# Eight softmax scalings and one diagonal moved from GpSimd to VectorE in a one-core decoder block

## The chip, the cores and the metric

The kernel runs on one core of one Trainium2 chip. The metric is the device time of one launch in microseconds (us). Five engines work side by side, each through its own list of instructions in a fixed order: TensorE (PE; its weight loads, PEld, have rows of their own), VectorE (DVE), ScalarE (ACT), GpSimd (POOL) and SyncE (SP), which here only issues transfers. An instruction that waits holds up all that stand behind it on its engine.

## The reference

One decoder block over 256 tokens of width 1024: norm, one q/k/v projection, two groups of eight attention heads, output projection, squared-ReLU MLP, a gated per-layer embedding, final norm. What the change touches is the norm ahead of the projection and the softmax of both groups:

```python
hn = rmsnorm(h, g_attn[i])            # y = x * rsqrt(mean(x*x) + EPS), times a gain
qkv = hn @ w_in[i]
...
scores = jnp.where(valid, scores + bias, -jnp.inf)      # group A, three dilations merged
lse = jax.nn.logsumexp(scores, axis=-1)
probs = jnp.exp(scores - lse[..., None])
...
sc = jnp.where(mask, sc - slopes * dist, -jnp.inf)      # group B
pr = jax.nn.softmax(sc, axis=-1)
out = jnp.einsum('bhqjk,bhqjkd->bhqd', pr, vg)
```

With 256 tokens each head's softmax is over at most 256 keys, so the kernel does it in two pieces of 128 queries (one with 256 keys, one with 128).

## The kernel before, in words

Every large product is done three times in fp32r: the operands are split into `hi` and `lo` halves and `mm3` (lines 151 to 155) multiplies hi by hi (L153), hi by the other's lo (L154) and lo by hi (L155). Weights arrive in slabs of 1 MB. Splitting a slab is cut into pieces: ScalarE makes `hi` (L75), VectorE makes `lo` from it (L76, `SCALAR_TENSOR_TENSOR`). The work is a list of units. While TensorE runs the steps of one unit, the pieces of the next unit's slabs are made. `inserts` names what is put between the steps: in `{4: [x_stats], 12: [x_bcast, ...]}` the statistics of x come behind step 4 and their broadcast behind step 12. An automatic scheduler then fixes the order of each engine's list.

**The diagonal.** GpSimd sums the squares of x (L253, L254) into `xsq`. `x_stats` adds them over the features on TensorE (L260), VectorE scales the sums (L185), GpSimd raises them to the power -1/2 (L186), and GpSimd multiplies the identity by the result, two tiles of 128x128 called `diag` (L267). `x_bcast` multiplies these on TensorE (L273) and VectorE copies the product to `rb` (L274), which scales every q and k (L287, L288). In the first q/k unit two output columns run side by side over k = 0 to 7. Steps 9 and 10 are the first to read the second of the unit's two slabs; its four `lo` pieces are made by VectorE directly behind L185.

**The scalings.** Heads go in pairs (g, j), group g = 0 or 1 and j = 0 to 3, eight pairs from (0,0) to (1,3). For a pair, `evac_qk` makes q and k with their halves (L287 to L294), `scores` multiplies them on TensorE (L316), VectorE adds the bias and takes the extremes (L322, L325), ScalarE does four exponentials with their sums (L331), VectorE takes the reciprocal of the four sums (L333), and GpSimd multiplies the four pieces of the probabilities `pb` by it in place (L337: 128x256 and 128x128 for each of two heads). `turn` then transposes `pb` on TensorE, three tiles for each head (L347), and `values` multiplies by v (L359, L360). GpSimd also makes the bias tables for later pairs (L304, and L306 for group 0), and those stand in its list between the scalings.

Of the kernel before, what the change touches and what calls it, by code (L numbers as in the profile page):

```python
# [14 lines left out]
ALU = mybir.AluOpType  # L15
# [17 lines left out]
def block_kernel(ctx: ExitStack, tc: tile.TileContext, a: dict):  # L33
    nc = tc.nc
# [8 lines left out]
    def bank():  # L43
        n_ps[0] += 1
        return psum.tile([P, 512], F32, tag="ps", name=f"ps{n_ps[0]}")
# [136 lines left out]
    def rstd_of(sums, n, width):  # L182

        ms, r = st(n), st(n)
        nc.vector.tensor_scalar(ms, sums, 1.0 / width, EPS, op0=ALU.mult, op1=ALU.add)  # L185
        nc.gpsimd.tensor_tensor(r, ms, mhalf[:, :n], op=ALU.pow)  # L186
        return r
# [35 lines left out]
    ident = outer.tile([P, P], F32, name="ident")  # L223
# [17 lines left out]
    xr = {}  # L241
# [14 lines left out]
    def sum_tokens(sums):  # L256

        ps = bank()
        for t in range(2):
            nc.tensor.matmul(ps[:, t : t + 1], sums[:, t * P : (t + 1) * P], ones[:, :1], start=True, stop=True)  # L260
        return ps[:, :2]

    def x_stats():
        xr["r"] = rstd_of(sum_tokens(xsq), 2, DM)
        diag = ap.tile([P, 2, P], F32, name="diag")
        for t in range(2):
            nc.gpsimd.tensor_scalar(diag[:, t], ident, xr["r"][:, t : t + 1], 1.0, op0=ALU.mult, op1=ALU.mult)  # L267
        xr["diag"] = diag

    def x_bcast():  # L270
# [37 lines left out]
    def scores(g, j):  # L308
        d = pr[g, j]

        ps = [bank(), bank()]
        for c, w, q0 in ((0, S, P), (S, P, 0)):
            for i, (a_, b_) in enumerate(((0, 0), (0, 1), (1, 0))):
                for h in range(2):
                    r = slice(h * HD, (h + 1) * HD)
                    last_mm[0] = nc.tensor.matmul(ps[h][:, c : c + w], d["q"][a_][r, q0 : q0 + P], d["k"][b_][r, :w],  # L316
                                                  start=i == 0, stop=i == 2)
        sc = ap.tile([P, 2, 3 * P], F32, tag="sc", name="sc", bufs=2)
        pb = d["p"] = ap.tile([P, 2, 3 * P], F32, tag="pb", name="pb", bufs=2)
        nm = ap.tile([P, 3, 4], F32, tag="nm", name="nm", bufs=3)  # L320
        for h in range(2):
            nc.vector.tensor_tensor_reduce(  # L322
                sc[:, h, P:], ps[h][:, :S], biases[g, j][:, h], 1.0, 3e38,
                op0=ALU.add, op1=ALU.min, accum_out=nm[:, 0, 2 * h : 2 * h + 1])
            nc.vector.tensor_tensor_reduce(  # L325
                sc[:, h, :P], ps[h][:, S : S + P], biases[g, j][:, h, P:], 1.0, 3e38,
                op0=ALU.add, op1=ALU.min, accum_out=nm[:, 0, 2 * h + 1 : 2 * h + 2])
        for h in range(2):
            for i, sl in ((0, slice(P, 3 * P)), (1, slice(0, P))):
                c = slice(2 * h + i, 2 * h + i + 1)  # L330
                nc.scalar.activation(pb[:, h, sl], sc[:, h, sl], AF.Exp, bias=nm[:, 0, c], scale=-1.0,  # L331
                                     accum_out=nm[:, 1, c])
        nc.vector.reciprocal(nm[:, 2], nm[:, 1])  # L333
        for h in range(2):
            for i, sl in ((0, slice(P, 3 * P)), (1, slice(0, P))):
                c = slice(2 * h + i, 2 * h + i + 1)
                nc.gpsimd.tensor_scalar(pb[:, h, sl], pb[:, h, sl], nm[:, 2, c], 1.0,  # L337
                                        op0=ALU.mult, op1=ALU.mult)

    def turn(g, j):  # L340
        d = pr[g, j]
# [84 lines left out]
    E_ = lambda g, j: (lambda: evac_qk(g, j, *qk_ps[g, j]))  # L426
    B_ = lambda g, j: (lambda: make_bias(g, j))
    S_ = lambda g, j: (lambda: scores(g, j))
    T_ = lambda g, j: (lambda: turn(g, j))
    V_ = lambda g, j: (lambda: values(g, j))  # L430
# [327 lines left out]
```

## Time and profile before

| | us |
|---|---|
| median of 3 runs | 351.51 (349.98 to 351.67) |
| the profiled execution, whole time | 348.54 |
| its span in the trace | 346.8 |
| TensorE busy | 331.6 (96%) |
| VectorE busy | 221.6 (64%) |
| ScalarE busy | 198.3 (57%) |
| GpSimd busy | 91.0 (26%) |

The profiled execution was 348.54 us, of which 1.7 us lie outside its span; it is 0.8% under the median of the three timed runs. The busy shares are means over stages: VectorE's 64% is made of stretches with over 90% and others with under half. Attention, where the change is, runs from about 23 to 105 us; from there on the products of the output projection and the MLP follow. Where the trace says that an engine waited for another, the row names the last of the events it waited for.

### The profile page before, as it was taken

The page shows a single profiled execution, that of the slowest core. Times are in us where ns is not written, and L with a number is a line of the kernel's source. Part 1 is how long each engine was busy: PE and PEld are TensorE (multiplying, and loading weights), DVE is VectorE, ACT ScalarE, POOL GpSimd, SP SyncE. Part 2 cuts the span into 40 slices and gives each one's busy share as a digit, 9 for nine tenths or more (in the row PEclk, how much of TensorE's full clock was granted, in tenths as well). Part 3 has the DMA queues.
Part 4 walks back from the last instruction along what each step waited for, and adds up shares of the span by engine and source line. Part 5 has one row for each costly group of instructions (what it writes and reads, how often), then busy time and mean ns, then how long its engine had stood idle before and what let it go on. Part 6 is the DMA issues. An engine that isn't in the chain of part 4 may idle for free.

```text
span 346.8 us, 5629 instructions
## 1 busy us (share of the span) xinstructions
PE 331.6 (96%) x2188; PEld 296.6 (86%) x2188; DVE 221.6 (64%) x371; ACT 198.3 (57%) x370; POOL 91.0 (26%) x120
## 2 busy tenths in 40 slices
PE   7899999999989999999999999999999999999990
PEld 6689889999866889898998988989989899888890
DVE  4898999786855669637537275293553843757563
ACT  5676667785783668738345374372652825458431
POOL 1887574554222001311010110110201102000443
PEclk9899999999999999999999999999999999999997
DMA  6996844435264078563737618356194472700011
GB/s 180 370 381 227 316 160 135 159 123 194 94 241 154 15 241 315 200 231 106 259 124 239 246 38 327 124 169 259 58 322 163 133 246 107 242 2 0 2 61 61
DMA packets 10827, 60.87 MB, mean 176 GB/s; under 512 B 1200, under 2 KB 1968, under 8 KB 4016
## 3 DMA queue, kind: packets, MB, share of 16 engines
q1 hardware_dynamic: 10800, 60.51, 49.5%
q8 instruction: 17, 0.28, 0.3%
q14 instruction: 10, 0.08, 0.1%
HBM read 59.46 MB, written 1.05 MB: 174 GB/s over the span
## 4 chain that ended last, share of the span: by engine, by line
PE 81%; POOL 7%; DVE 5%; ACT 2%; issue 2%; DMA 2%; SPq 1%; POOLq 0%; DVEq 0%; ACTq 0%
PE ps L153 26%; PE ps L154 25%; PE ps L155 25%; DVE lo L76 3%; POOL xsq L254 2%; POOL pb L337 2%; DMA xT<-in_xT 2%; POOL sq L253 1%; PE ps L359 1%; PE ps L316 1%; PE ps L347 1%; ACT pb L331 1%; PE ps L476 1%; PE ps L360 1%; SPq L212 0%
## 5 line engine op out<-in xcount | busy, mean ns | idle before, releaser
L76 DVE SCALAR_TENSOR_TENSOR lo<-raw,head,hi 128x512 fp32r<-128x512 f32 (+2 forms) x137 | 109.8, 851 | 24.3 <-ACT hi L75 24.2
L75 ACT ACTIVATE hi<-raw,head 128x512 fp32r<-128x512 f32 (+2 forms) x137 | 92.6, 734 | 26.0 <-PE ps L154 11.2
L153 PE MATMUL ps<-hhi,hi 128*128 128x256 f32 x256 | 72.6, 283 | 0.0
L155 PE MATMUL ps<-hhi,lo 128*128 128x256 f32 x256 | 72.4, 283 | 0.0
L154 PE MATMUL ps<-hlo,hi 128*128 128x256 f32 x256 | 72.4, 283 | 0.0
L84 DVE TENSOR_TENSOR lo<-raw,hi 128x1024 fp32r<-128x1024 f32 x34 | 41.5, 1254 | 28.1 <-ACT hi L83 28.0
L540 POOL TENSOR_TENSOR sq<-r 128x512 f32<-128x512 f32 (+1 forms) x18 | 19.9, 1107 | 141.8 <-ACT r L538 141.8
L153 PE MATMUL ps<-hi,u 128*128 128x512 f32 x128 | 50.2, 392 | 0.0
L83 ACT ACTIVATE hi<-raw 128x1024 fp32r<-128x1024 f32 x34 | 34.3, 1052 | 27.2 <-PE ps L155 25.5
L154 PE MATMUL ps<-lo,u 128*128 128x512 f32 x128 | 49.9, 390 | 0.0
L155 PE MATMUL ps<-hi,u 128*128 128x512 f32 x128 | 49.8, 389 | 0.0
L153 PEld LDWEIGHTS ps<-hhi,hi 128*128 128x128 f32 x256 | 49.1, 192 | 0.3
L154 PEld LDWEIGHTS ps<-hlo,hi 128*128 128x128 f32 x256 | 49.1, 192 | 0.3
L155 PEld LDWEIGHTS ps<-hhi,lo 128*128 128x128 f32 x256 | 49.1, 192 | 0.0
L153 PE MATMUL ps<-xhi,hi 128*128 128x256 f32 x128 | 37.8, 297 | 0.0
L154 PE MATMUL ps<-xlo,hi 128*128 128x256 f32 x128 | 36.0, 282 | 0.0
L155 PE MATMUL ps<-xhi,lo 128*128 128x256 f32 x128 | 35.4, 282 | 0.0
L543 DVE TENSOR_TENSOR u<-sq,u 128x512 fp32r<-128x512 f32 (+1 forms) x18 | 11.7, 651 | 34.0 <-ACT u L542 34.0
L155 PEld LDWEIGHTS ps<-hi,u 128*128 128x128 f32 x128 | 24.0, 188 | 5.0
L153 PEld LDWEIGHTS ps<-hi,u 128*128 128x128 f32 x128 | 24.1, 188 | 4.7
L154 PEld LDWEIGHTS ps<-lo,u 128*128 128x128 f32 x128 | 24.1, 188 | 4.7
L153 PEld LDWEIGHTS ps<-xhi,hi 128*128 128x128 f32 x128 | 24.4, 191 | 1.2 <-issue 0.7
(128 smaller groups left out, 540.2 us busy)
## 6 DMA issues: line engine op xcount, KB each, us to landing
raw<-in_w_up SPq DMA_DIRECT2D x16, 1024.0 KB, 5.0
raw<-in_w_down SPq DMA_DIRECT2D x16, 1024.0 KB, 4.8
raw<-in_w_in SPq DMA_DIRECT2D x10, 1024.0 KB, 6.3
raw<-in_w_out SPq DMA_DIRECT2D x4, 1024.0 KB, 4.8
raw<-in_w_gate SPq DMA_DIRECT2D x4, 1024.0 KB, 4.9
raw<-in_w_in SPq DMA_DIRECT2D x7, 256.0 KB, 6.7
h_sb<-in_x SPq DMA_DIRECT2D x1, 1024.0 KB, 7.2
raw<-in_w_ple SPq DMA_DIRECT2D x1, 1024.0 KB, 4.9
```

What stands on the lines that cost most here:

```text
L75: nc.scalar.activation(h, r, AF.Copy, scale=sc)
L76: nc.vector.scalar_tensor_tensor(l, r, sc, h.bitcast(F32), op0=ALU.mult, op1=ALU.subtract)
L83: nc.scalar.activation(h, r, AF.Copy)
L84: nc.vector.tensor_tensor(l, r, h.bitcast(F32), op=ALU.subtract)
L153: nc.tensor.matmul(ps, lhs[0], rhs[0], start=start, stop=False)
L154: nc.tensor.matmul(ps, lhs[0], rhs[1], start=False, stop=False)
L155: last_mm[0] = nc.tensor.matmul(ps, lhs[1], rhs[0], start=False, stop=stop)
L253: nc.gpsimd.tensor_tensor(sq, x, x, op=ALU.mult)
L254: nc.gpsimd.tensor_tensor(xsq, xsq, sq, op=ALU.add)
L337: nc.gpsimd.tensor_scalar(pb[:, h, sl], pb[:, h, sl], nm[:, 2, c], 1.0, op0=ALU.mult, op1=ALU.mult)
L540: nc.gpsimd.tensor_tensor(sq, r, r, op=ALU.mult)
L543: nc.vector.tensor_tensor(o[1], sq, o[0].bitcast(F32), op=ALU.subtract)
```

## The change

The two multiplications of the identity and the four multiplications of each pair's probabilities are issued on VectorE, as `tensor_scalar` with one operation (the form on GpSimd had a second multiplication by 1.0):

```diff
         for t in range(2):
-            nc.gpsimd.tensor_scalar(diag[:, t], ident, xr["r"][:, t : t + 1], 1.0, op0=ALU.mult, op1=ALU.mult)
+            nc.vector.tensor_scalar(diag[:, t], ident, xr["r"][:, t : t + 1], None, op0=ALU.mult)
...
                 c = slice(2 * h + i, 2 * h + i + 1)
-                nc.gpsimd.tensor_scalar(pb[:, h, sl], pb[:, h, sl], nm[:, 2, c], 1.0,
-                                        op0=ALU.mult, op1=ALU.mult)
+                nc.vector.tensor_scalar(pb[:, h, sl], pb[:, h, sl], nm[:, 2, c], None, op0=ALU.mult)
```

GpSimd loses 34 instructions and VectorE gains 34; every shape stays. TensorE's list and the transfers keep their order. Lines behind the edit carry a number that is lower by one.

VectorE, about the statistics of x (`stat` holds them, `lo` are the pieces of weight slabs, `rb` the broadcast):

```order
 L76 SCALAR_TENSOR_TENSOR lo<-raw,head,hi 128x512 x5
 L185 TENSOR_SCALAR stat<-ps_303 128x2
+L267 TENSOR_SCALAR diag<-ident,stat 128x128 x2
 L76 SCALAR_TENSOR_TENSOR lo<-raw,head,hi 128x512 x4
 L274 COPY rb<-ps_339 128x256
```

The two diagonal products, which need the result of GpSimd's L186, now stand ahead of the four `lo` pieces of the second slab.

VectorE, from the softmax of pair (0,0) on (`q` and `k` are those of pair (0,1), `nm` holds the sums and their reciprocals):

```order
 L292 TENSOR_TENSOR q<-q 128x256
 L333 RECIPROCAL nm<-nm 128x4
+L337 TENSOR_SCALAR pb<-pb,nm 128x256
+L337 TENSOR_SCALAR pb<-pb,nm 128x128
+L337 TENSOR_SCALAR pb<-pb,nm 128x256
+L337 TENSOR_SCALAR pb<-pb,nm 128x128
 L294 TENSOR_TENSOR k<-k 128x256
 L76 SCALAR_TENSOR_TENSOR lo<-raw,head,hi 128x512 x5
```

The four scalings follow the reciprocal and stand ahead of the `lo` half of the next pair's k and of five slab pieces.

GpSimd, the same place (bias tables and scalings of group 0):

```order
 L304 TENSOR_SCALAR bias<-consts 128x256 x2
 L306 TENSOR_TENSOR bias<-bias,consts 128x256 x2
-L337 TENSOR_SCALAR pb<-pb,nm 128x256
-L337 TENSOR_SCALAR pb<-pb,nm 128x128
-L337 TENSOR_SCALAR pb<-pb,nm 128x256
-L337 TENSOR_SCALAR pb<-pb,nm 128x128
 L304 TENSOR_SCALAR bias<-consts 128x256 x2
 L306 TENSOR_TENSOR bias<-bias,consts 128x256 x2
```

GpSimd's scalings stood behind the bias table of a later pair; now its list holds the bias tables one after the other.

## Rows read from the trace of the kernel before

**Rows 1.** Page, part 1: busy us, share, instructions of each engine

```profile
PE 331.6 (96%) x2188; PEld 296.6 (86%) x2188; DVE 221.6 (64%) x371; ACT 198.3 (57%) x370; POOL 91.0 (26%) x120
```

**Rows 2.** TensorE's waits, whole span: us in total, times, longest

```profile
PE ps L347 <- POOL pb L337: 2.8, 3, 1.2
PE ps L153 <- ACT xhi L219: 2.4, 2, 1.8
PE ps L164 <- DVE mhalf L174: 1.0, 1, 1.0
PE ps L260 <- POOL xsq L254: 0.8, 1, 0.8
```

**Rows 3.** Waits of TensorE's weight loads, 20 to 124 us, one row

```profile
PEld ps L273 <- POOL diag L267: 0.3, 1, 0.3
```

**Rows 4.** Timeline of TensorE: start us, us, instructions [idle before <- releaser]

```profile
25.29 0.40 PE L155 MATMUL ps<-xhi,lo 128*128 128x256 f32 x2
...
26.01 0.40 PE L155 MATMUL ps<-xhi,lo 128*128 128x256 f32 x2
26.49 0.83 PE L273 MATMUL ps<-diag,ones 128*128 128x128 f32 x4
...
40.50 0.91 PE L316 MATMUL ps<-k,q 64*128 64x256 f32 x12
42.38 0.55 PE L347 MATMUL ps<-ident,pb 128*128 128x128 f32 x3 [0.43 <-POOL pb L337]
44.04 0.55 PE L347 MATMUL ps<-ident,pb 128*128 128x128 f32 x3 [1.11 <-POOL pb L337]
...
97.75 0.55 PE L347 MATMUL ps<-ident,pb 128*128 128x128 f32 x3
99.52 0.55 PE L347 MATMUL ps<-ident,pb 128*128 128x128 f32 x3 [1.22 <-POOL pb L337]
```

**Rows 5.** Timeline of GpSimd, same columns

```profile
23.70 1.17 POOL L186 TENSOR_TENSOR stat<-stat,mhalf 128x2 f32<-128x2 f32 x1 [0.94 <-DVE stat L185]
24.98 1.81 POOL L267 TENSOR_SCALAR diag<-ident,stat 128x128 f32<-128x128 f32 x2
26.87 0.89 POOL L304 TENSOR_SCALAR bias<-consts 128x256 f32<-128x256 f32 x2
...
39.04 1.61 POOL L306 TENSOR_TENSOR bias<-bias,consts 128x256 f32<-128x256 f32 x2
40.65 3.34 POOL L337 TENSOR_SCALAR pb<-pb,nm 128x256 f32<-128x256 f32 x4
...
54.37 2.48 POOL L337 TENSOR_SCALAR pb<-pb,nm 128x256 f32<-128x256 f32 x4 [0.72 <-DVE nm L333]
...
96.87 2.60 POOL L337 TENSOR_SCALAR pb<-pb,nm 128x256 f32<-128x256 f32 x4 [7.34 <-DVE nm L333]
```

**Rows 6.** Timeline of VectorE, same columns

```profile
17.77 5.55 DVE L76 SCALAR_TENSOR_TENSOR lo<-raw,head,hi 128x512 fp32r<-128x512 f32 x5
23.46 0.16 DVE L185 TENSOR_SCALAR stat<-ps 128x2 f32<-128x2 f32 x1
23.54 2.74 DVE L76 SCALAR_TENSOR_TENSOR lo<-raw,head,hi 128x512 fp32r<-128x512 f32 x4
...
39.10 0.18 DVE L333 RECIPROCAL nm<-nm 128x4 f32<-128x4 f32 x1 [0.40 <-ACT pb L331]
39.41 0.65 DVE L294 TENSOR_TENSOR k<-k 128x256 fp32r<-128x256 f32 x1
40.03 4.50 DVE L76 SCALAR_TENSOR_TENSOR lo<-raw,head,hi 128x512 fp32r<-128x512 f32 x5
...
96.53 0.18 DVE L333 RECIPROCAL nm<-nm 128x4 f32<-128x4 f32 x1 [0.76 <-ACT pb L331]
97.94 2.59 DVE L76 SCALAR_TENSOR_TENSOR lo<-raw,head,hi 128x1024 fp32r<-128x1024 f32 x2 [1.24 <-ACT hi L75]
```

**Rows 7.** VectorE's groups by shape: busy us, mean ns of one | idle before

```profile
L677 DVE TENSOR_SCALAR hg<-hg,stat 128x512 f32<-128x512 f32 x2 | 1.0, 488 | 1.3 <-POOL stat L675 1.3
L185 DVE TENSOR_SCALAR stat<-ps 128x2 f32<-128x2 f32 x3 | 0.5, 155 | 1.8 <-PE ps L260 1.6
```

**Rows 8.** Timeline of the end of the kernel: VectorE and GpSimd side by side

```profile
342.37 0.49 DVE L677 TENSOR_SCALAR hg<-hg,stat 128x512 f32<-128x512 f32 x1 [0.67 <-POOL stat L675]
342.44 0.75 POOL L680 TENSOR_SCALAR hg<-hg,stat 128x256 f32<-128x256 f32 x1
```

**Rows 9.** Three stretches of attention: us, busy us (instructions) of each engine, clock

```profile
40.00:55.00 15.00, 13.46 (x118) 12.17 (x118) 13.82 (x37) 10.68 (x32) 10.86 (x17) 1.00 0.64 227
...
sum 44.00, PE 42.46 PEld 39.12 DVE 37.15 ACT 31.21 POOL 26.82; mean PE 14.15 PEld 13.04 DVE 12.38 ACT 10.40 POOL 8.94
```

**Rows 10.** The chain that ended last, one piece: transposes of pair (0,2)

```profile
60.05 0.66 PE ps L347 x6
```

## Prediction

> **What bounds the kernel now.** I read the page's busy shares first: TensorE works 331.6 of 346.8 us [rows 1], so a change elsewhere can only give back time in which TensorE stands still, or cost some. Next its waits over the whole span [rows 2]: four kinds, 7.0 us together. Two of these belong to the start (x's split, the warm-up) and one to the sum of squares ahead of the statistics; the change leaves them alone. The fourth, 2.8 us in three waits, is for the scaled probabilities. The weight loads add 0.3 us in front of the diagonal's product [rows 3]. So the most that this change can take away directly is 2.8 + 0.3 = 3.1 us. The timeline shows where the three are [rows 4]: 0.43 and 1.11 us at the transposes of pair (0,0), 1.22 us at those of pair (1,3). The other six pairs have none: pair (0,2), for one, is scaled by 54.37 + 2.48 = 56.85 us and transposed at 60.05 [rows 5, 10]. From about 105 us on TensorE has no wait among the four, so what is won by then should stay won to the end.
>
> **Part 1, the scalings.** For pair (0,0) the reciprocal is done at 39.10 + 0.18 = 39.28 us [rows 6], but GpSimd first finishes a later bias table (39.04 + 1.61 = 40.65), then scales for 3.34 us, to 43.99 [rows 5]: 4.7 us after the reciprocal. For pair (1,3) nothing is queued ahead, and it is 2.60 us from 96.87 on, to 99.47, 2.8 us after the reciprocal's end at 96.71.
>
> No scaling on VectorE is in the trace. The nearest rows are its two `tensor_scalar` forms [rows 7]: 155 ns for 128x2 and 488 ns for 128x512. On a line between them, 128x128 is 155 + 333 x 126/510 = 237 ns and 128x256 is 155 + 333 x 254/510 = 321 ns, so a pair's four are 2 x 0.237 + 2 x 0.321 = 1.12 us. If every one cost what the smaller row or the larger one costs, it is 0.62 or 1.95 us. I take 1.12, since both shapes lie between the rows and operation and engine are the same; only the source of the smaller row, PSUM, differs.
>
> Pair (0,0) is then scaled at about 39.28 + 1.12 = 40.4 us, before the 41.95 us at which TensorE would reach its transposes (42.38 - 0.43). Both waits go: **-1.54 us**. Pair (1,3): 96.71 + 1.12 = 97.83. The first head's half is done by 97.27, ahead of 97.75, and the second head's by 97.83, while TensorE would reach it near 98.30 (99.52 - 1.22). That wait goes too: **-1.22 us**. The list behind it is not hurt there, since the pieces at 97.94 idled 1.24 us for ScalarE anyway [rows 6]. What is late next at both places is nothing but TensorE's own list.
>
> The cover: the other six pairs gain nothing, and add 1.12 us each to VectorE. In 40 to 84 us VectorE is busy 37.15 of 44 us [rows 9], so 6.85 us are free; six pairs add 6.7. What makes it fit is that VectorE is slowed by GpSimd today: five slab pieces beside the scalings of pair (0,0) took 4.50 us, 0.90 each, against 2.74/4 = 0.69 at 23.54 us [rows 6], so that pair gives back 5 x 0.21 = 1.1 us. And the transposes have room: 3.2 us for pair (0,2), as above. I cost these six at nothing. If that cover were gone, they would cost what is over, which is the last rival below.
>
> One thing behind the scalings is tight: the k half of pair (0,1) (L294), whose scores start at 40.50 us. It ended at 39.41 + 0.65 = 40.06; behind the scalings and without its own slowing it ends at about 40.4 + 0.4 = 40.8. Part 2 moves TensorE's need to about 41.2, so I put +0.1 us here, between nothing and the rival's 1.2.
>
> By the Trainium skill ("SBUF — State Buffer", section "Who interferes with whom") a VectorE `tensor_scalar` in its two-port mode and a GpSimd instruction exclude one another: the one that starts first keeps the shared ports for its whole length. The trace agrees at the one place that shows it: a GpSimd 128x256 that started 0.07 us after VectorE's 0.49 us `tensor_scalar` took 0.75 us [rows 8], against 0.89/2 = 0.45 each for the bias tables of that shape [rows 5]. That speaks against the move wherever GpSimd still makes bias tables; the sum by it is the second rival's.
>
> **Part 2, the diagonal.** It saves GpSimd 1.81 us, and the 0.3 us that TensorE's weight load waited. But look at VectorE's list: the two products now stand between L185 and four slab pieces, and they need GpSimd's power, done at 23.70 + 1.17 = 24.87 us [rows 5]. Before, VectorE started those pieces at 23.54 and did not wait [rows 6]. Now it stands still from 23.62 to 24.87, and the first piece comes after 24.87 + 2 x 0.24 + 0.69 = 26.04 us instead of 24.23. TensorE's first use of that piece is the L155 pair at 25.29 us, the next piece's is at 26.01 [rows 4]. So there is **a new wait**. In addition GpSimd, free of the diagonal, starts its bias tables at 24.87 instead of 26.87 and runs beside VectorE's pieces; pieces beside GpSimd took 0.90 (above) to 5.55/5 = 1.11 us [rows 6]. I take 0.25 us more: 26.3, that is 1.0 us after 25.29. Bounds: diagonal products of 0.155 us and a piece of 0.69 give 25.87, +0.6 us; products of 0.488, a bias operation of 0.45 in front and a piece of 1.11 give 27.4, +2.1, and as pieces 1.11 apart are used 0.72 apart, the second costs 0.4 more: +2.5. I stay near the lower end, because the pieces at 23.54 themselves ran at 0.69 while GpSimd's diagonal tried to run beside them. With the 0.3 us gone at the diagonal's own product, part 2 costs **+0.7 us** (0.3 to 2.2).
>
> **Sum.** -1.54 - 1.22 + 0.1 + 0.7 = -1.96, say -2.0 us. The profiled execution took 348.54 us (346.8 of span), so 346.5 us. The timed runs lie higher, median 351.51; the same ratio, 346.5/348.54 = 0.9943, gives 349.5 us, which I predict.
>
> **Rivals.**
> *The diagonal costs more.* If the pieces come 1.11 us apart, part 2 is +2.2 and the sum -2.76 + 0.1 + 2.2 = -0.5: 348.1 profiled, 351.0 median. For it: pieces at 17.77 us did run at 1.11 [rows 6]. Against: those ran beside two-input GpSimd work.
> *GpSimd's bias tables block the scalings.* At pair (0,0) the two L306 take 1.61 us. If the four scalings wait out both, they end at 39.28 + 1.61 + 1.12 = 42.0 and the k half at 42.4, against scores wanted at 41.2: +1.2 in place of +0.1, sum -0.9, 347.6 profiled, 350.6 median. Against: the bias tables start earlier now too.
> *No new wait.* If another instruction or a later need hides the first piece, only 0.3 is gained in part 2: -3.0, 348.5 median. Against: the order and the 25.29 us row leave no cover.
> *The move does not remove the waits,* because exponentials or something else end last at the same place: then part 2 alone counts, +0.7, 352.2 median. Against: the reciprocal was done 4.7 and 2.8 us before the scalings ended.
> *VectorE becomes the bound, and it is slower.* With 1.95 us for a pair, six add 11.7 us to 37.15: 48.9 in 44, 4.9 us too many, and -2.0 + 4.9 = +2.9: 351.4 profiled, 354.4 median. It decides once a pair costs over 6.85/6 = 1.14 us net of what GpSimd's absence gives back. For it: 13.82 of 15 us are busy from 40 to 55 [rows 9]. Against: the 3 us of room, and the slowing that goes.
>
> **How the numbers follow.** Chances: forecast 0.52, costlier diagonal 0.15, blocked scalings 0.12, no new wait 0.08, waits stay 0.05, VectorE bound 0.08. About 0.5% (1.75 us) is what a measurement of this kernel can tell from no change. The forecast lies just beyond that bound, so its 0.52 splits into 0.38 faster and 0.14 same; no new wait is all faster; the costlier diagonal and the blocked scalings are 0.25 same and 0.02 faster; waits that stay count 0.04 same and 0.01 slower; the bound VectorE is slower. Faster 0.48, same 0.43, slower 0.09. The range takes in the forecast with its bounds, both dearer cases and the missing wait, with about 0.4 us for the spread of runs: 347.9 to 351.6.
>
> **What would show it.** Right: no wait of L347 for the scalings; VectorE idle about 1.25 us in front of the diagonal, by GpSimd's power; a new wait of TensorE's L155 near 25.3 us of about 1 us, for a slab piece; scalings of 0.24 and 0.32 us; slab pieces near 41 us at about 0.7. Wrong: L155 near 25.3 without a wait, scores (L316) waiting for the k half from 40 us on, or VectorE without idle time from 40 to 84 us while TensorE waits for it.

## The result, and the profile after

The changed kernel takes 347.47 us (median of six runs, 347.12 to 348.55), against 350.56 us for the kernel before (six runs, the three shown ahead among them, 348.62 to 351.67). The ratio is 0.9924, with a 95% interval of 0.9901 to 0.9947. The forecast ratio, 0.9943, lies in that interval; the forecast time, 349.5 us with a range of 347.9 to 351.6, missed the measured one: it is 0.4 us below the range's lower end. One run of the kernel before, beside the last experiments, took 409.92 us at a mean granted clock of 0.752 instead of about 0.99; it is left out of the medians here.

Part 1 of the page shows the work that moved: VectorE has 34 instructions more than before and GpSimd 34 fewer, and 5.8 us more of VectorE's time stand against 23.2 us less of GpSimd's [rows 1].

```profile
PE 332.2 (96%) x2188; PEld 298.2 (86%) x2188; DVE 227.4 (66%) x405; ACT 197.8 (57%) x370; POOL 67.8 (20%) x86
```

TensorE's waits over the whole span in the profiled execution of the changed kernel (us in total, times, longest) no longer have the row for `pb`, which was 2.8 us in three waits [rows 2]:

```profile
PE ps L260 <- POOL xsq L254: 1.9, 1, 1.9
PE ps L153 <- ACT xhi L219: 1.8, 1, 1.8
...
PE ps L155 <- DVE xlo L220: 0.8, 2, 0.5
```

Two things in this list need care. The wait at L260, the sums of squares ahead of the statistics, has grown from 0.8 to 1.9 us, though the change lies behind it. And the new wait that the prediction expects, L155 for a piece of the slab's `lo`, is missing. The stretches of this trace (us, then busy us and instructions of PE, PEld, DVE, ACT, POOL, then TensorE's granted clock, DMA share, GB/s) say why that place can't be read here: for 3.4 us right behind L260 the granted clock is 0.51, the lower of TensorE's two levels (1.2 instead of 2.4 GHz), and TensorE is busy without a gap.

```profile
23.80:27.20 3.40, 3.40 (x17) 3.40 (x17) 2.09 (x5) 1.93 (x4) 2.43 (x4) 0.51 0.94 349
```

In the trace of before the same kind of stretch lay earlier:

```profile
11.60:15.00 3.40, 3.40 (x9) 2.62 (x10) 3.40 (x4) 2.94 (x5) 3.40 (x4) 0.50 1.05 417
```

So more executions of both kernels were profiled, the kernels unchanged. In the third trace of the changed kernel this place is undisturbed. Its timelines (start us, us, instructions, idle time before and what released it), TensorE first, to be held against [rows 4]:

```profile
23.56 0.61 PE L260 MATMUL ps<-ones,xsq 128*128 128x1 f32 x4 [0.80 <-POOL xsq L254]
...
26.53 0.51 PE L155 MATMUL ps<-xhi,lo 128*128 128x256 f32 x2 [0.35 <-DVE lo L76]
...
29.62 0.38 PE L155 MATMUL ps<-xhi,lo 128*128 128x256 f32 x1 [0.17 <-DVE lo L76]
...
42.09 1.16 PE L316 MATMUL ps<-k,q 64*128 64x256 f32 x12
43.65 0.82 PE L346 MATMUL ps<-ident,pb 128*128 128x128 f32 x6
...
98.02 0.92 PE L346 MATMUL ps<-ident,pb 128*128 128x128 f32 x6
...
337.34 0.28 PE L155 MATMUL ps<-hi,glo 128*128 128x256 f32 x1
```

The transposes (now line 346) of pairs (0,0) and (1,3), at 43.65 and 98.02 us, run as one group of six with nothing in brackets. The new wait is there: 0.35 us at 26.53, 0.17 at 29.62. VectorE, of the same trace, against [rows 6]:

```profile
25.20 0.63 DVE L267 TENSOR_SCALAR diag<-ident,stat 128x128 f32<-128x128 f32 x2 [0.83 <-POOL stat L186]
25.74 3.83 DVE L76 SCALAR_TENSOR_TENSOR lo<-raw,head,hi 128x512 fp32r<-128x512 f32 x4
...
40.31 1.76 DVE L337 TENSOR_SCALAR pb<-pb,nm 128x256 f32<-128x256 f32 x4
41.99 0.41 DVE L294 TENSOR_TENSOR k<-k 128x256 fp32r<-128x256 f32 x1
42.33 3.39 DVE L76 SCALAR_TENSOR_TENSOR lo<-raw,head,hi 128x512 fp32r<-128x512 f32 x5
...
97.33 1.01 DVE L337 TENSOR_SCALAR pb<-pb,nm 128x256 f32<-128x256 f32 x4
```

VectorE stands still for 0.83 us until GpSimd has made the power, then makes the diagonal in 0.63 us, and its four slab pieces take 3.83 us, 0.96 each, where they took 2.74/4 = 0.69 before. The four are not alike: the first takes 0.74 us by itself, the last two together (a narrower window of the same view):

```profile
27.20 2.36 DVE L76 SCALAR_TENSOR_TENSOR lo<-raw,head,hi 128x512 fp32r<-128x512 f32 x2
```

The scalings of pair (0,0) take 1.76 us, those of pair (1,3) 1.01 us. What GpSimd does beside the first two, against [rows 5]:

```profile
24.44 0.72 POOL L186 TENSOR_TENSOR stat<-stat,mhalf 128x2 f32<-128x2 f32 x1 [0.94 <-DVE stat L185]
25.25 1.50 POOL L304 TENSOR_SCALAR bias<-consts 128x256 f32<-128x256 f32 x2
26.83 2.19 POOL L306 TENSOR_TENSOR bias<-bias,consts 128x256 f32<-128x256 f32 x2
...
40.04 1.49 POOL L306 TENSOR_TENSOR bias<-bias,consts 128x256 f32<-128x256 f32 x2
```

The bias tables run beside the slab pieces at 25.74 and beside the scalings at 40.31.

**From the sums to the last product.** A comparison that the start doesn't disturb needs two marks that every kernel here has: the first product of the sums (L260) and the last product of all (L155 on `glo`). Kernel before, first trace:

```profile
22.82 0.61 PE L260 MATMUL ps<-ones,xsq 128*128 128x1 f32 x4 [0.80 <-POOL xsq L254]
...
338.48 0.28 PE L155 MATMUL ps<-hi,glo 128*128 128x256 f32 x1
```

The difference is 338.48 - 22.82 = 315.66 us. The same subtraction on all traces of the two kernels:

| trace | time (us) | L260 starts | last L155 starts | between |
|---|---|---|---|---|
| before, first | 348.54 | 22.82 | 338.48 | 315.66 |
| before, second | 349.14 | 23.43 | 339.08 | 315.65 |
| before, third | 349.46 | 23.74 | 339.41 | 315.67 |
| changed, first (lower clock behind L260) | 347.48 | 23.50 | 337.41 | 313.91 |
| changed, second | 347.50 | 23.70 | 337.44 | 313.74 |
| changed, third | 347.44 | 23.56 | 337.34 | 313.78 |

Between the marks three executions of before agree within 0.02 us. Their own times differ by 0.92 us, and so do their starts of L260 (22.82 to 23.74): all of the difference between these three arises ahead of the sums. The change is worth 313.74 to 313.91 less 315.66, that is -1.9 us (-1.75 to -1.92). The prediction's sum was -1.96. That the two agree is partly luck: its terms, held one by one against the table at the end of the experiments, are off in both directions.

### The profile page after: what moved, and what is told of

It is laid out like the page before. It is cut to its first block, busy times and chain, and to the rows that moved or that the text cites. A ratio compares the mean times of both kernels' runs of the same rounds, so it can differ in the third digit from the quotient of the medians.

```text
span 345.7 us, 5613 instructions
## 1 busy us (share of the span) xinstructions
PE 332.2 (96%) x2188; PEld 298.2 (86%) x2188; DVE 227.4 (66%) x405; ACT 197.8 (57%) x370; POOL 67.8 (20%) x86
## 4 chain that ended last, share of the span: by engine, by line
PE 91%; POOL 4%; DMA 2%; SPq 1%; DVE 1%; issue 0%; POOLq 0%; ACT 0%; DVEq 0%
PE ps L153 29%; PE ps L154 28%; PE ps L155 28%; POOL xsq L254 2%; PE ps L316 2%; DMA xT<-in_xT 2%; POOL sq L253 2%; PE ps L346 2%; PE ps L358 1%; PE ps L475 1%; PE ps L359 1%; SPq L212 0%; PE ps L260 0%; POOLq L753 0%; POOL stat L674 0%
## 5 line engine op out<-in xcount | busy, mean ns | idle before, releaser
L76 DVE SCALAR_TENSOR_TENSOR lo<-raw,head,hi 128x512 fp32r<-128x512 f32 (+2 forms) x137 | 108.7, 843 | 22.1 <-ACT hi L75 21.7
L153 PE MATMUL ps<-hhi,hi 128*128 128x256 f32 x256 | 72.6, 283 | 0.0
L155 PE MATMUL ps<-hhi,lo 128*128 128x256 f32 x256 | 72.5, 283 | 0.0
L153 PE MATMUL ps<-hi,u 128*128 128x512 f32 x128 | 50.2, 392 | 0.0
L83 ACT ACTIVATE hi<-raw 128x1024 fp32r<-128x1024 f32 x34 | 34.3, 1052 | 27.2 <-PE ps L155 25.5
L155 PE MATMUL ps<-hi,u 128*128 128x512 f32 x128 | 49.8, 389 | 0.0
L153 PEld LDWEIGHTS ps<-hhi,hi 128*128 128x128 f32 x256 | 49.1, 192 | 0.3
L155 PEld LDWEIGHTS ps<-hhi,lo 128*128 128x128 f32 x256 | 49.1, 192 | 0.0
L153 PE MATMUL ps<-xhi,hi 128*128 128x256 f32 x128 | 38.6, 303 | 0.0
L155 PE MATMUL ps<-xhi,lo 128*128 128x256 f32 x128 | 36.0, 286 | 0.0
L155 PEld LDWEIGHTS ps<-hi,u 128*128 128x128 f32 x128 | 24.0, 188 | 5.1
L153 PEld LDWEIGHTS ps<-hi,u 128*128 128x128 f32 x128 | 24.1, 188 | 4.7
L153 PEld LDWEIGHTS ps<-xhi,hi 128*128 128x128 f32 x128 | 25.2, 197 | 1.2 <-issue 0.7
```

What stands on the lines that cost most here:

```text
L76: nc.vector.scalar_tensor_tensor(l, r, sc, h.bitcast(F32), op0=ALU.mult, op1=ALU.subtract)
L83: nc.scalar.activation(h, r, AF.Copy)
L153: nc.tensor.matmul(ps, lhs[0], rhs[0], start=start, stop=False)
L155: last_mm[0] = nc.tensor.matmul(ps, lhs[1], rhs[0], start=False, stop=stop)
```

## The experiments

The ratios below stand against runs of the kernel before that were made on the same chip in turn: its median was 349.10 us (347.69 to 351.17) beside the first four experiments, 349.18 (347.78 to 351.49) beside the next four, 349.30 beside the last. "Between" is the stretch of the table above.

**Only the scalings on VectorE.** The diagonal goes back to GpSimd:

```
 for t in range(2):
-    nc.vector.tensor_scalar(diag[:, t], ident, xr["r"][:, t : t + 1], None, op0=ALU.mult)
+    nc.gpsimd.tensor_scalar(diag[:, t], ident, xr["r"][:, t : t + 1], 1.0, op0=ALU.mult, op1=ALU.mult)
```

> Only the scalings of the probabilities go to VectorE; the diagonal stays on GpSimd, so on VectorE the four slab pieces follow L185 at once. Theory A (the diagonal on VectorE costs 0.7 us, because it stands in front of the slab pieces): this kernel is 0.7 us faster than the changed one, -2.7 us against before, near 347.8 us where before is 350.5, and no wait of the first L155 behind the statistics. Theory B (the diagonal costs nothing, the piece is hidden or the start makes it up): equal to the changed kernel within 0.3 us, -2.7 us against before as the changed kernel itself. In both, the three waits of L346 for the scalings are gone. The two theories are told apart by this kernel beside the copy of the changed one in the same call.

Measured: 347.32 us, ratio 0.9939 (0.9915 to 0.9963); between 336.39 - 22.86 = 313.53 us, -2.13 against before. TensorE's timeline:

```profile
22.86 0.60 PE L260 MATMUL ps<-ones,xsq 128*128 128x1 f32 x4 [0.91 <-POOL xsq L254]
...
40.53 0.39 PE L316 MATMUL ps<-k,q 64*128 64x256 f32 x2
41.51 0.79 PE L316 MATMUL ps<-k,q 64*128 64x256 f32 x10 [0.59 <-DVE k L294]
42.70 0.82 PE L346 MATMUL ps<-ident,pb 128*128 128x128 f32 x6
...
97.07 0.92 PE L346 MATMUL ps<-ident,pb 128*128 128x128 f32 x6
```

VectorE's, of the same kernel:

```profile
39.36 1.77 DVE L337 TENSOR_SCALAR pb<-pb,nm 128x256 f32<-128x256 f32 x4
41.04 0.41 DVE L294 TENSOR_TENSOR k<-k 128x256 fp32r<-128x256 f32 x1
```

All three waits for `pb` are gone, 2.76 us by [rows 4], and one of 0.59 us has come: the scores of pair (0,1) stop after two products for the k half, which ends at 41.45 behind the four scalings. 2.76 - 0.59 = 2.17 looks like the 2.13, but this is chance: the waits that went were worth more than their brackets and something between them was lost (the table at the end of the experiments). Counted between the table's marks, the wait for the k half alone is 0.80. The scalings took 1.77 us rather than the 1.12 of the estimate, which puts the k half 0.65 us later, which is most of that wait.

**Only the diagonal on VectorE.** The scalings go back to GpSimd, the diagonal stays as in the change:

```
-                nc.vector.tensor_scalar(pb[:, h, sl], pb[:, h, sl], nm[:, 2, c], None, op0=ALU.mult)
+                nc.gpsimd.tensor_scalar(pb[:, h, sl], pb[:, h, sl], nm[:, 2, c], 1.0,
+                                        op0=ALU.mult, op1=ALU.mult)
```

> Only the diagonal goes to VectorE; the probabilities stay on GpSimd. Theory A: TensorE comes 0.7 us late out of the first q/k unit, and VectorE's softmax of pair (0,0) too, so the transposes of that pair keep their 1.5 us of wait: +0.5 to +1.0 us against before. Theory B: within 0.3 us of before. The row to read is the first L155 behind the statistics and what VectorE idles for in front of L267.

Measured: 349.06 us, ratio 0.9988 (0.9969 to 1.0008); between 338.79 - 23.17 = 315.62, -0.04 against before. TensorE's waits:

```profile
PE ps L347 <- POOL pb L337: 2.2, 2, 1.1
...
PE ps L155 <- DVE lo L76: 0.5, 2, 0.3
```

The scores of pair (0,1) start 41.73 - 23.17 = 18.56 us behind L260, against 40.50 - 22.82 = 17.68 before: the diagonal costs 0.88 us there. None of it arrives at the end, because it is spent where TensorE had to wait anyway: the waits for `pb` fall from 2.8 to 2.2 us, the first of them (0.43) vanishing, and counted between marks they give back 0.62 us at pair (0,0) and 0.24 at pair (1,3). Here a delay ahead of a wait cost nothing as far as the wait could take it up.

**Only two pairs on VectorE.** The scalings of pairs (0,0) and (1,3), where TensorE waited, go to VectorE; those of the other six and the diagonal stay on GpSimd:

```
+                if (g, j) in ((0, 0), (1, 3)):
+                    nc.vector.tensor_scalar(pb[:, h, sl], pb[:, h, sl], nm[:, 2, c], None, op0=ALU.mult)
+                else:
+                    nc.gpsimd.tensor_scalar(pb[:, h, sl], pb[:, h, sl], nm[:, 2, c], 1.0, ...
```

> Only pairs (0,0) and (1,3) are scaled on VectorE, the other six and the diagonal on GpSimd. If only those two places matter, as the prediction says, this kernel equals the one with all eight pairs on VectorE and the diagonal on GpSimd, -2.7 us against before. If VectorE's freed time beside GpSimd's scalings matters elsewhere, or the six others cost something on VectorE, the two differ by more than 0.5 us.

Measured: 346.87 us, ratio 0.9938 (0.9913 to 0.9964); between 336.31 - 22.70 = 313.61, within 0.1 us of the kernel with all eight pairs on VectorE. TensorE's waits there:

```profile
PE ps L316 <- DVE k L294: 0.6, 1, 0.6
PE ps L350 <- POOL pb L340: 0.5, 1, 0.5
```

The 0.6 us for the k half are the same. A 0.5 us wait is new: the second head of pair (0,1) waits for GpSimd's scaling. The kernel before has no such wait; TensorE now comes to these transposes 1.1 us earlier (50.63 - 22.70 = 27.93 us behind L260, 51.84 - 22.82 = 29.02 in before). TensorE's transposes of pair (1,3), which end the stretch of the six pairs:

```profile
97.10 0.82 PE L350 MATMUL ps<-ident,pb 128*128 128x128 f32 x6
```

So the six other pairs make no difference of more than 0.1 us between the engines, but not because they are hidden: part of the lead that TensorE has won at pair (0,0) is lost among them on either engine, 0.57 us here and 0.39 with all scalings on VectorE (the table at the end of the experiments).

**The changed kernel again**, beside these three on the same chip:

> The changed kernel itself, for comparison in the same call and for a second trace of the start. Theory A: a wait of 0.5 to 1.1 us of the first L155 behind the statistics whenever TensorE runs that stretch at its upper clock level. Theory C (the start varies from run to run more than the diagonal costs): the time at which the sums (L260) start and the stretch at the lower clock level lie elsewhere than in the first trace (23.5 us and 23.5 to 27.2 us).

Measured: 347.34 us, ratio 0.9946 (0.9925 to 0.9967); between 313.74. In its trace L260 again waits 1.9 us, yet no stretch at the lower clock follows, and the new wait of L155 is there (0.36 and 0.17 us). So the late sums don't hide that wait. In the first trace the stretch at the lower clock stands in its place: 17 products in 3.4 us, where the third trace has 25 in the same 3.4 us and has to wait.

**The diagonal on ScalarE.** If the 0.88 us come from VectorE's standing still for GpSimd's power, an engine with nothing due at this place should take the diagonal for less. All scalings stay on VectorE:

```
-            nc.vector.tensor_scalar(diag[:, t], ident, xr["r"][:, t : t + 1], None, op0=ALU.mult)
+            nc.scalar.activation(diag[:, t], ident, AF.Copy, scale=xr["r"][:, t : t + 1])
```

> All scalings on VectorE as in the change, the diagonal on ScalarE (activation Copy with scale), where it stands behind eight slab pieces and in front of the copies of v, which wait for the same power. VectorE does not stand still behind L185. If it is the stop of VectorE for GpSimd's power that makes the slab pieces late in the changed kernel, no L155 waits for a slab piece behind the statistics here, and the first q/k unit is as fast from L260 on as before. By the time this equals the kernel with only the scalings on VectorE: 0.9939 of before, 0.2 to 0.3 us faster than the change; and scores of pair (0,1) wait 0.6 us for the k half, as there.

Measured: 345.84 us, ratio 0.9909 (0.9882 to 0.9937); between 336.23 - 23.35 = 312.88, -2.78 against before and 0.9 us better than the change. Made a second time on another chip:

> The same kernel as diag_act, again, beside k_first_2 on one chip. From L260 to the last product 312.9 us again, 2.8 us less than before (315.66 us in both traces of before) and 0.9 to 1.0 us less than the changed kernel; 0.991 of before.

Measured: 346.53 us, ratio 0.9928 (0.9902 to 0.9953); between 335.64 - 22.74 = 312.90. The expectation was too modest: against the kernel with only the scalings moved, which it was to equal, 312.90 is 0.63 us shorter. And one thing more has changed than the edit says: the scheduler has put TensorE's four diagonal products (L273) behind four more products of the slabs, in two pairs; in the other kernels with the diagonal on GpSimd or VectorE, TensorE's order is that of before. ScalarE's timeline in this second one:

```profile
24.82 0.70 ACT L267 ACTIVATE diag<-ident,stat 128x128 f32<-128x128 f32 x2 [2.47 <-POOL stat L186]
```

VectorE's, of the same trace:

```profile
23.46 2.88 DVE L76 SCALAR_TENSOR_TENSOR lo<-raw,head,hi 128x512 fp32r<-128x512 f32 x4
```

TensorE's, with the pair of L155 that had to wait in the change, ahead of the products whose place has changed:

```profile
25.20 0.40 PE L155 MATMUL ps<-xhi,lo 128*128 128x256 f32 x2
...
39.93 0.39 PE L316 MATMUL ps<-k,q 64*128 64x256 f32 x2
...
96.30 0.92 PE L346 MATMUL ps<-ident,pb 128*128 128x128 f32 x6
```

ScalarE waits 2.47 us for the same power, and TensorE's list shows no wait for its diagonal; VectorE's pieces are back at 2.88/4 = 0.72 us each, straight behind L185. The pair of L155 comes 25.20 - 22.74 = 2.46 us behind L260, as before (25.29 - 22.82 = 2.47); with the diagonal on VectorE it is 26.53 - 23.56 = 2.97. So the cost comes from the diagonal's place in VectorE's queue: the pieces stand behind an instruction that itself waits. The first wait of L155 is the halt (0.83) and the products (0.63) together, since the first piece takes 0.74 us in the change and 0.75 in before; the later one stands behind the two pieces of 2.36/2 = 1.18 us, beside GpSimd's two-input bias tables.

The scores start 39.93 - 22.74 = 17.19 us behind L260, 0.49 earlier than even before. There TensorE's weight load waited 0.29 us for GpSimd's diagonal and the four products took 0.83 us [rows 3, 4], where they take 0.39 + 0.38 here. How much of the 0.49 is the earlier diagonal and how much the later place of its products, no run tells apart.

**The k half ahead of the scalings.** What is left of a wait in that kernel is 0.42 us at the scores of pair (0,1). Here the scalings of pair (0,0) are a function of their own, called later, so that VectorE makes the k half behind the first of four:

```
+        if (g, j) != (0, 0):
+            scale_p(g, j)
...
-             {0: [E_(0, 1), late_loads], ...
+             {0: [E_(0, 1), Z_(0, 0), late_loads], ...
```

> As diag_act, but the scalings of pair (0,0) are written behind the q and k of pair (0,1), so that the k half (L294) stands behind the first of the four scalings instead of behind all four. Theory: the scalings in front of the k half cost 0.6 us at the scores of pair (0,1); here that wait is gone, the transposes of pair (0,0) still do not wait, and the time is 0.6 us under diag_act: about 0.992 of before. Rival: the wait only moves, to the transposes (scalings later) or to the slab pieces, and the time equals diag_act.

> The same kernel as k_first, again. In its first trace the stretch from the sums (L260) to the scores of pair (0,1) fell into the lower clock level; from the thirteenth matmul behind the diagonal's product on it was 0.6 us shorter than diag_act. Theory: without that stretch L316 has no wait for the k half, and from L260 to the last product of the slabs it is 0.4 to 0.6 us shorter than diag_act (312.9 us there), median 0.4 to 0.6 us lower. Rival: no difference.

Measured: 346.39 us, ratio 0.9925 (0.9903 to 0.9948), and on the other chip 346.38, ratio 0.9910 (0.9883 to 0.9937). The first trace has 3.4 us at the lower clock from 24.4 on, behind sums that were 1.93 us late, and 338.11 - 24.20 = 313.91 between; the second is undisturbed, 336.03 - 23.10 = 312.93. That is no better than the 312.88 and 312.90 without it. TensorE's timeline of the second shows where it went:

```profile
40.32 0.98 PE L316 MATMUL ps<-k,q 64*128 64x256 f32 x12
41.69 0.82 PE L352 MATMUL ps<-ident,pb 128*128 128x128 f32 x6
...
47.08 0.65 PE L364 MATMUL ps<-pT,vt 128*64 128x256 f32 x2
...
47.88 0.39 PE L153 MATMUL ps<-xhi,hi 128*128 128x256 f32 x1
```

The same places with the diagonal on ScalarE alone (second trace):

```profile
40.74 0.79 PE L316 MATMUL ps<-k,q 64*128 64x256 f32 x10 [0.42 <-DVE k L294]
41.93 0.82 PE L346 MATMUL ps<-ident,pb 128*128 128x128 f32 x6
...
47.46 0.38 PE L153 MATMUL ps<-xhi,hi 128*128 128x256 f32 x1
```

Counted from L260, the transposes start 0.6 us earlier (41.69 - 23.10 = 18.59 against 41.93 - 22.74 = 19.19), and the product behind the values is no earlier (24.78 against 24.72): the values of pair (0,0) split in two halves, and the second starts just behind ScalarE's copy of its transposed probabilities, which ends at 46.57 + 0.46 = 47.03:

```profile
46.57 0.46 ACT L354 COPY pT<-ps 128x384 f32<-128x384 f32 x1
```

The wait only moved on by 5 us.

**The scalings made twice.** The kernel with only the scalings moved, each piece multiplied once more, by 1.0:

```
                 nc.vector.tensor_scalar(pb[:, h, sl], pb[:, h, sl], nm[:, 2, c], None, op0=ALU.mult)
+                nc.vector.tensor_scalar(pb[:, h, sl], pb[:, h, sl], 1.0, None, op0=ALU.mult)
```

> Every scaled piece is multiplied once more, by 1.0, on VectorE; the diagonal is on GpSimd. This adds another 1.1 to 1.3 us for each of the eight pairs. If the six inner pairs are hidden, as the prediction says, only two places pay: the k half of pair (0,1) is 1.1 to 1.3 us later and so are the scores that wait for it, and at pair (1,3) the transposes wait up to 0.6 us: +1.2 to +1.9 us against the kernel with only the scalings moved, near or under before. Rival (VectorE is at its limit from 40 to 84 us): each of six pairs adds its 1.1 us, +6 us or more, 1% slower than before.

Measured: 349.35 us, ratio 0.9994 (0.9969 to 1.0019); between 339.66 - 23.84 = 315.82, +2.29 against the same kernel with one scaling. TensorE's timeline:

```profile
43.17 0.79 PE L316 MATMUL ps<-k,q 64*128 64x256 f32 x10 [1.26 <-DVE k L294]
```

Its three stretches of attention, as in [rows 9], the sum of 44 us:

```profile
sum 44.00, PE 42.16 PEld 38.78 DVE 42.13 ACT 29.58 POOL 10.04; mean PE 14.05 PEld 12.93 DVE 14.04 ACT 9.86 POOL 3.35
```

and those of the third trace of the changed kernel:

```profile
40.00:55.00 15.00, 15.00 (x133) 14.03 (x132) 14.79 (x44) 10.47 (x31) 4.56 (x8) 1.00 0.62 220
...
sum 44.00, PE 44.00 PEld 41.08 DVE 40.48 ACT 31.35 POOL 10.12; mean PE 14.67 PEld 13.69 DVE 13.49 ACT 10.45 POOL 3.37
```

With the change VectorE still has 3.5 us free in these 44, though only 0.2 in the first 15. Twice the scalings fill 42.1 of 44, and then TensorE does wait: 0.7 us more for the k half (1.26 for 0.59), the rest behind it. So VectorE as a whole is not the bound with one scaling, though single places in these 44 us are (below); with another 11.5 us of such work (6.1 + 5.4 us by the groups below) it begins to be.

**Both kernels once more**, one execution each:

> The kernel before itself, for a second trace of its start. Question: do the time at which the sums of the statistics start (22.8 us in the first trace, 23.5 and 23.7 in the two of the changed kernel) and the stretch at the lower clock level (11.6 to 15.0 us) come again? If these vary from run to run by themselves, up to about 1 us each, the timed runs of one kernel spread by some 2 us without any change, as they do (347.7 to 351.2).

> The kernel before, third trace. From L260 to the last product 315.66 us, as in the two others to 0.01 us, whatever the start does; the wait ahead of L260 0.8 to 0.9 us if the change matters for it, 0.8 or 1.9 if it is chance.

> The changed kernel, third trace. In its two others TensorE waited 1.9 us for GpSimd's sums ahead of L260, in both traces of before 0.8 and 0.9 us. If that is chance of the start, it can be 0.9 here; if the change brings it, 1.9 again. From L260 to the last product: 313.75 us, if no stretch at the lower clock level lies behind L260.

Measured: 349.14, 349.46 and 347.44 us, the table's second, third and last rows. They settle that the stretch between the marks repeats to a few hundredths of a microsecond, and that what varies lies ahead of it.

**Where the differences arise.** Brackets can't be added up: in the trace of before, TensorE's products of L153 to L155 start 0.12 us apart and are shown 0.28 us long, so a bracket leaves out the first 0.16 us of a pause. Starts of the same product in two kernels can be compared. Four stretches, from the rows above and [rows 4] (the end of the transposes is the start of their last group plus its length):

| us | before | changed, third trace | scalings only | two pairs | diagonal only | diagonal on ScalarE, second trace |
|---|---|---|---|---|---|---|
| L260 to scores of pair (0,1) | 17.68 | +0.85 | -0.01 | 0.00 | +0.88 | -0.49 |
| to the end of the transposes of (0,0) | 4.09 | -1.71 | -1.10 | -1.10 | -0.62 | -1.27 |
| to the start of the transposes of (1,3) | 53.16 | +0.39 | +0.39 | +0.57 | -0.06 | +0.39 |
| to the last product | 240.73 | -1.41 | -1.41 | -1.52 | -0.24 | -1.39 |
| sum | 315.66 | -1.88 | -2.13 | -2.05 | -0.04 | -2.76 |

The second stretch holds the waits for `pb` at pair (0,0) and the wait for the k half. In the kernel with the k half ahead, which shows neither, it is 41.69 + 0.82 - 40.32 = 2.19 us. So the two waits for `pb` cost 4.09 - 2.19 = 1.90 us rather than their brackets' 1.54, and the k half costs 2.38 - 2.19 = 0.19 in the change and 2.99 - 2.19 = 0.80 with the scalings alone.

The third stretch is that of the six other pairs, and there the three kernels of the table with all scalings on VectorE lose 0.39 us each. One place shows how. With the scalings alone, ScalarE's copy and TensorE's weight loads for the values of pair (0,2):

```profile
62.44 0.46 ACT L348 COPY pT<-ps 128x384 f32<-128x384 f32 x1
```

```profile
62.95 0.19 PEld L358 LDWEIGHTS ps<-pT,vt 128*64 128x64 f32 x2
```

The second head's loads start right behind the copy's end at 62.90. That copy stands behind the exponentials of pair (0,3), and these behind VectorE's bias and extremes, which VectorE, busy without a gap, begins 60.15 - 22.86 = 37.29 us behind L260, as in before (60.10 - 22.82 = 37.28): TensorE's lead of 1.1 us doesn't reach VectorE. Whether this is the scalings' own time or the rest of VectorE's work, no run tells apart.

## Why the prediction missed its time

**The waits that go (-1.54 and -1.22): right, and priced too low.** TensorE's list of waits has none for VectorE's `pb` in any kernel with all scalings there. By the table they were worth 1.90 and 1.41 us, 0.55 more than the brackets together.

**The price of a scaling: right alone, too low beside GpSimd.** Four took 1.01 us at pair (1,3) against 1.12 estimated, but 1.76 at pair (0,0), beside a bias table. Over all eight pairs, VectorE's groups by shape in the third trace of the changed kernel (busy us, mean ns of one), against the 237 and 321 ns worked out from [rows 7]:

```profile
L337 DVE TENSOR_SCALAR pb<-pb,nm 128x256 f32<-128x256 f32 x16 | 6.1, 379 | 0.2
L337 DVE TENSOR_SCALAR pb<-pb,nm 128x128 f32<-128x128 f32 x16 | 5.4, 340 | 0.0
```

The Trainium skill ("SBUF — State Buffer", section "Who interferes with whom") has a VectorE `tensor_scalar` in its two-port mode and a GpSimd instruction shut one another out where they overlap. The 1.76 us beside the table against 1.01 without one agree in direction; the 0.75 us between them are half of the table's 1.49. Whether these scalings ran in that mode, no trace shows.

**The k half of pair (0,1) (+0.1, bounds 0 to 1.2): nearly right in the change, mis-sized by itself.** In the change it costs about 0.2 us, because TensorE comes 0.85 us later; with the scalings alone it was 0.8 (0.59 in the bracket). This is the rival "GpSimd's bias tables block the scalings" in part: the scalings ended 1.77 us after they could start, where the estimate had 1.12 and that rival 1.61 + 1.12 = 2.73.

**The six other pairs (0): too low.** Two pairs moved or eight, the whole is 313.61 or 313.53 us, but the stretch of the six costs 0.39 us with all scalings on VectorE. The slab pieces behind pair (0,0) fell to 3.39/5 = 0.68 us each, as the prediction said (about 0.7), which gives back 1.1 us.

**The diagonal (+0.7): right at its place, made up otherwise.** The wait is there, VectorE stands still ahead of it (0.83 us, 1.25 forecast: GpSimd's power took 0.72 us and not 1.17), and the scores start 0.85 us later in the change. Of this 0.5 (2.97 - 2.47) is the first wait, where 1.0 was forecast; the rest comes from the later pieces, which the forecast left out, less what the diagonal's own products gain. In the full change that delay and the k half's overlap: a TensorE that comes later finds more of the k half done. Alone they cost 0.88 and 0.80 us, together 0.85 + 0.19 = 1.04, where the prediction had 0.7 + 0.1 = 0.8.

**The sum (-1.96): right, partly by luck.** By the table it is -1.90 - 1.41 + 0.19 + 0.39 + 0.85 = -1.88. The gains were forecast 0.55 us too small and the costs 0.63 us too small, and the two cancel.

**The rivals.** "The waits stay" and "no new wait" fall with the rows above. "The diagonal costs more" (+2.2 at L155) falls with 0.88. "VectorE becomes the bound" falls with the twofold scalings: even twice the work cost 2.3 us and not the 4.9 that one scaling at 1.95 us a pair was to cost, and one scaling leaves 3.5 of 44 us free. A pair's scalings do take 11.5/8 = 1.44 us, over the 1.14 that the rival names, but VectorE's work in the 44 us grew by 40.48 - 37.15 = 3.33 us only. The 0.39 us of the third stretch are what is left of this rival.

**The step that failed: the last, from the sum to a time.** The prediction carried -1.96 us by a ratio onto the median of three runs, 351.51, and let the spread of runs widen the range by only about 0.4 us (0.6 by its own ends, 348.5 - 347.9). That median was high: later medians of the kernel before were 350.56, 349.10, 349.18 and 349.30, and single runs went from 347.69 to 351.67. With 349.1 to 349.3 the same sum gives 347.1 to 347.3; measured were 347.3 to 347.5. The prediction had the two numbers that warned of it, a profiled execution at 348.54 beside a median of 351.51, 3.0 us apart, and used a ratio where it should have widened the range by that distance: from its 346.5 to its 349.5. Neither end alone was the time: 346.5 is 1 us low, since the profiled execution has the earliest start of L260 (22.82) of the three of before. The side came out as the likeliest of the three chances, faster by 0.76%.

**What stays open.** Why the start takes from 22.70 to 24.20 us in these traces is settled in part. TensorE's first product that waits for ScalarE's `xhi` behind 9 us (L153) starts at 10.14, 10.74 and 11.06 us in the three traces of before, and L260 12.68 or 12.69 us behind it in all three; ScalarE's L219 in turn waits there for the transfer of x. So the spread of before comes from when that piece of x arrives, and why this differs is open. In some (the changed kernel's first two, the first of the kernel with the k half ahead) the sums wait 1.9 us for GpSimd rather than 0.8 or 0.9; in some a 3.4 us stretch runs at the lower clock. Both occur apart from one another: the second trace of the changed kernel has the late sums without a low stretch, the first of before a low stretch without late sums. Nor does any trace show an execution near 351 us, so where those lose their 2 us is not known.

## What to carry to other kernels

Before an operation is moved to another engine, look at who makes its operand and at what stands behind it in the new queue: the diagonal's power comes from GpSimd, so on VectorE it puts a 0.83 us halt in front of four pieces that TensorE needs, while on ScalarE, which waits there for the same power anyway, it made nothing late that shows and gave the shortest stretch here (312.88 and 312.90 us). Count a delay only at the end of the list, since the next wait absorbs it (0.88 us became 0.2), count a wait from start to start rather than by its bracket (1.90 for 1.54 us), and a wait removed by reordering may just turn up 5 us later. When a change is worth 2 us and the profiled execution and the median of three runs lie 3 us apart, forecast the difference from the trace and let the range span both.

## What the runs showed that was not expected

- A stretch of 3.4 us at the lower of TensorE's two clock levels comes at the kernel's start in some executions and not in others, at places that change: 11.6 to 15.0 us in the first trace of before, none in its second and third (in the third, 11.60 to 15.00 us ran at 1.00), 23.8 to 27.2 in the first of the changed kernel, none in its second, 12.1 to 15.6 in its third; six of the fourteen traces have one. Ahead of the stretch at 23.8 TensorE had stood still for 1.93 us; in the second trace it stood still as long and the clock stayed. Its price depends on what lies under it: nothing at 11.6 us (the 12.68 us to L260 above are the same with it and without), 0.15 us in the changed kernel (313.91 for 313.76), where L155 would have waited for its slab piece anyway, and 1.0 us in the kernel with the k half ahead (313.91 for 312.93).
- The same VectorE instructions vary by what GpSimd does beside them: four scalings 1.01 or 1.76 us, four slab pieces 2.88 us with the diagonal on ScalarE and 3.83 us behind the diagonal on VectorE. Beside the latter GpSimd makes bias tables from 25.25 to 29.02 us, so nearly all through; beside the former only from 24.88 us on, when half of the pieces were done.
